# The first mixer's projections and attention waves in another order

## The chip, the cores and the metric

The program runs on one core of a Trainium2 chip. The metric is the device time of one execution in microseconds (us); the time before is the median of three runs. The engines are named PE (TensorE), ACT (ScalarE), DVE (VectorE), POOL (GpSimd) and SP (SyncE, which issues most of the DMAs). "Granted clock" is the share of full speed at which TensorE was allowed to run in a stretch: 1.00 is the upper of its two levels, 2.4 GHz, and a mean below it means that part of the stretch ran at the lower, 1.2 GHz.

## The reference, cut to what matters

Two layers, each a mixer and a feed-forward part, over 512 tokens of width 1024. The change touches the mixer of the first layer: one input projection gives the gate and the input of a recurrent unit, queries, six key and value tensors, and gates; attention sums three branches.

```python
h = modulate(x, norm_mix, sh_m, sc_m)
(a_gate, a_x, q, kc, vc, ks, vs, kw, vw, gts) = _split(h @ w_in, IN0_SIZES)
y_a = rg_lru(causal_conv(a_x, conv_w, conv_b), wa, ba, wx, bx, lam) * jax.nn.gelu(a_gate)
...
        o = gc[..., 0:1] * o_cmp + gc[..., 1:2] * o_slc + gc[..., 2:3] * o_win
...
x = x + g_m[:, None, :] * (jnp.concatenate([y_a, y_b], axis=-1) @ w_out)
```

`o_cmp` attends to 31 compressed blocks, `o_slc` to selected blocks, `o_win` to a window. With 512 tokens the selection and the window take every earlier token, so the kernel computes branches 1 and 2 as plain causal attention. The modulation values (`sh_m`, `sc_m`, `g_m` and so on) are six products of one vector with a 1024x1024 matrix.

## The kernel before

All matrix products are float32 in three passes (`passes`, L382 to L390): high part by high part (L387), low by high (L388), high by low (L389). A weight block of 1024x256 comes by one DMA of 1 MB (`load_next`, L163) into one of four buffers `raw`, is split into `whi` (ACT, L173) and `wlo` (DVE or POOL, L174), and gives two output tiles of 128x512, with 24 matmuls of 128x512 for each.

The order of the weights is the list `entries`, filled at L679: `win` (keys and values of branch 2, called the third branch in the change's name, since the compressed one is branch 0), `gts` (gates), `q0`, `q1`, `ax0`, `ax1` (recurrent input), `ag0`, `ag1` (recurrent gate), then four blocks of the output projection. `MIX_MODS` (L38) says how many blocks of the modulation matrices are loaded behind each of them; each such block costs TensorE 16 small matmuls (L256), ACT a copy `mrow` (L259) and TensorE the sum L267.

What runs when is decided by `Weaver` (L40), a co-operative scheduler: generators hand it pieces of work with estimated lengths and waits, and it writes them out by priority; a pass that follows then fixes the order on every engine. `backbone` (L1167) is the generator of the projections. It first ends the four tiles of the first two key/value blocks (banks `b_mm`, `b_mm`, `b_sc`, `b_sc`), then takes the `win` block on two banks `b_o`, then the gates (`gts_unit`, L1056), the two query blocks and the recurrent unit. Each of those tiles is emptied by ACT and DVE: `cmp_evac` (L932: `kc2`, ACT L939 and DVE L940, then `kb` on POOL, L947), `dup_k` (L1017: `khi` on ACT, `klo` on DVE) and `v_rows` (L1031: `vf` on ACT, four transposes L1040 on TensorE, the copy `vt1` or `vt2` on DVE, L1042). `compress` (L953) makes the compressed keys from `kb`.

Attention is another generator, `att_run` (L560). It works through units of one query block of 128 queries, one branch and some heads: scores into one of two banks `b_sc` (L499, L500, mask L510), maximum `negm` (DVE L515), exponential `pr` (ACT L518), normalisation (DVE L523 to L527), transposes (L534) and products with the values (L555). The list `waves` sets the order of the units: for each query block first branch 1, then branch 2. The recurrent unit is `lru1` (a convolution `xc`: ACT L865, three DVE passes L867), `lru_gates` (matmuls L875 and L877, ACT L880 and L881) and `lru2`.

Of the kernel before, what the change touches and what calls it, by code (L numbers as in the profile page):

```python
# [34 lines left out]
FFN_MODS = (((0, 1, "wu"), (0, 2, "wg"), (0, 2, "wu"), (0, 3, "wg"), (0, 0), (0, 1), (0, 2), (0, 3), (1, 0, "wg"), (1, 0, "wu"), (1, 1, "wg"), (1, 1, "wu"), (1, 2, "wg"), (1, 2, "wu"), (1, 3, "wg"), (1, 3, "wu"),   # L35
             (1, 0), (1, 1), (1, 2), (1, 3), (2, 0, "wg"), (2, 0, "wu"), (2, 1, "wg"), (2, 1, "wu"), (2, 2, "wg"), (2, 2, "wu"),  (2, 0), (2, 1)),
            ())
MIX_MODS = {'win': 0, 'gts': 0, 'q0': 2, 'q1': 1, 'ax0': 1, 'ax1': 2, 'ag0': 3, 'ag1': 2, 0: 1, 1: 0, 2: 0, 3: 0}  # L38
NPT0, OSB, NPR = 3, 2, 4
PIECES = ((4, 4, 3), (4, 4, 3))  # L40

# [56 lines left out]
def trunk(ctx, tc, I, out):  # L98
# [461 lines left out]
    def att_run(A, pre):  # L560

        flat, act, dve = [], 0.0, 0.0
        per = {0: 4, 1: 2, 2: 1, 3: 1}
        brs, ng = A["brs"], A["ng"]
        tail = brs[-1]
        waves = [(qb, w) for qb in range(NB) for w in range(0, ng, 4 if qb < 2 else 2)]
        if ng > 4:
            waves = [(qb, w) for w in (0, 4) for qb in (0, 1)] + [v for v in waves if v[0] > 1]
        for qb, w in waves:
            n, nh = per[qb], (4 if qb < 2 else 2)  # L570
            for br in brs:
                for z in range(2):
                    for h in range(w, w + nh, n):
                        hs = [z * ng + h + j for j in range(n)]
                        ev = (br, w, nh) if z == 1 and h + n == w + nh else None
                        flat.append((qb, br, z, w, h - w, nh, hs, ev))
        live, obank, pvq = {}, {}, []
        n_u = len(flat)
        for i in range(n_u + 3):
            todo, pvq = pvq, []  # L580
            if 0 <= i - 2 < n_u:
                qb, br, z, w, j0, nh, hs, ev = flat[i - 2]
                pt, W, n, ready = live.pop(i - 2)
                if ready > wv.now:
                    yield ("wait", ready - wv.now)
                pick = A["late"] is None and dve <= act
                if j0 == 0:
                    A["PT"][qb, br, w, z] = A["pool"].tile([P, 1024], F32, name="pT", tag="pT", bufs=A["npT"])[:, :nh * W]
                pe = att_T(pt, A["PT"][qb, br, w, z][:, j0 * W:(j0 + n) * W], W, n, pick)
                t0 = wv.now + pe + 100.0  # L590
                if pick:
                    dve = done = max(dve, t0) + 130.0 + n * W * 1.04
                else:
                    act = done = max(act, t0) + 220.0 + n * W * 0.83
                if ev is not None:
                    pvq = [(qb, ev, done + 100.0)]
                yield pe
            if i < n_u:
                qb, br, _, _, _, _, hs, _ = flat[i]
                for f in pre(qb, hs):  # L600
                    yield ("until", f)
                if (qb, br) in A["hooks"]:
                    wv.spawn(A["hooks"].pop((qb, br))(), -3)
                pt, pe, W, n = att_unit(A, qb, br, hs, i % 2)
                late = A["late"] is not None
                dve = max(dve, wv.now + pe + 100.0) + 130.0 + n * W * 1.04
                act = max(act, dve + 100.0) + n * (230.0 + W * 0.83)
                if i % 2 and not late:
                    dve = max(dve, act) + 400.0 + 2 * n * (100.0 + W * 0.52)
                    live[i - 1] = live[i - 1][:3] + (dve + 100.0,)  # L610
                live[i] = (pt, W, n, (act if late else dve) + 100.0)
                yield pe
            for qb, (br, w, nh), ready in todo:
                if ready > wv.now:
                    yield ("wait", ready - wv.now)
                hb = (qb, w // 4)
                if hb not in obank:
                    obank[hb] = bank("o")
                first = br == brs[0]
                if first and A["cmp"] is not None:  # L620
                    yield ("until", ("cmpo", qb))
                    yield att_PV(A, qb, 0, w, nh, obank[hb], True, False)
                    first = False
                yield att_PV(A, qb, br, w, nh, obank[hb], first, br == tail)
                if br == tail and (w + nh) % 4 == 0:
                    A["done"](qb, w // 4, obank.pop(hb))
# [48 lines left out]
    add_mod(0, 0, 2, None)  # L675
    add_mod(0, 1, 3, None)
    add_mod(0, 0, 3, None)
    for nm, c0 in (("win", 2048), ("gts", 2304), ("q0", 1024), ("q1", 1280), ("ax0", 512), ("ax1", 768), ("ag0", 0),
                   ("ag1", 256)):  # L679
        if nm == "gts":  # L680
            entries.append(("h", ("in0", nm), W0, 0, KT, c0, 24, None))
        else:
            add_w(("in0", nm), W0, 0, KT, c0, 256, (P, P))
        emit_mods(dve_mods, MIX_MODS[nm])
# [162 lines left out]
    def layer0():  # L847
# [201 lines left out]
        def kv_evac(br):  # L1049
            def f(n, o, t0, t1):  # L1050
                if n == 0:
                    dup_k(Ks, br, o, mp, "kk", 2)
                else:
                    v_rows(Vs, br, o, mp, "xc", 2)
            return f
# [76 lines left out]
        def done(qb, half, o):  # L1132
# [6 lines left out]
                 cmp=lambda qb, i: (CK["v"][:, i % 2].rearrange("p z d -> p (z d)"),  # L1139
                                    PCT[qb][:, (i // 2) * P:(i // 2 + 1) * P]),  # L1140
                 late=None, hooks={(qb, 1): (lambda qb=qb: cmp_block(qb)) for qb in range(NB)})
        wv.spawn(att_run(A, lambda qb, hs: [("q", 7), "gts", "cmp"]), -1)

        def ag_evac(ft, o):
            ag = mp.tile([P, S], F32, name="ag", tag="xc", bufs=2)
# [19 lines left out]
        sq_ = stack_q(Qs, mp, "qs", 8, 0.125, lambda h: h // 4)  # L1165

        def backbone():  # L1167
            need(("in0", "win"))
            for n, ev in enumerate((cmp_evac, kv_evac(1))):
                for z in range(2):  # L1170
                    for k in kv_g[2 * n + z]:
                        yield 3 * MM
                    ev(z, kv_o[2 * n + z], 0, S)
            for y in pair(("in0", "win"), KT, 2, rh, rl, ("o", "o"), kv_evac(2)):
                yield y
            wv.set("kv2", CMP_WAIT)
            for y in gts_unit(("in0", "gts")):
                yield y
            for j in range(2):
                def qe(n, o, t0, t1, j=j):  # L1180
                    sq_(4 * j + 2 * n, o)
                    wv.set(("q", 4 * j + 2 * n), 2000.0)
                    wv.set(("q", 4 * j + 2 * n + 1), 2500.0)
                for y in pair(("in0", "q%d" % j), KT, 2, rh, rl, T2, qe):
                    yield y
            for j in range(2):
                for y in pair(("in0", "ax%d" % j), KT, 2, rh, rl, T2, lambda n, o, t0, t1, j=j: lru1(2 * j + n, o)):
                    yield y
                if j:
                    yield ("until", ("lru", 0))  # L1190
                for ft in (2 * j, 2 * j + 1):
                    yield ("until", ("xc", ft))
                    for y in lru_gates(ft):
                        yield y
                wv.spawn(lru2(j), -4)
# [243 lines left out]
    def layer1():  # L1439
# [88 lines left out]
        def done(qb, half, o):  # L1528
# [5 lines left out]
            for p in range(4):  # L1534
                for z in range(2):
# [8 lines left out]
        A = dict(pool=mp, npr=3, bias=BIAS, K=Ks, Q=Qs, V=Vs, PT={}, npT=3, ng=8, grp=lambda h: h // 8, done=done, brs=(3,),  # L1544
                 gate=None, cmp=None, hooks={},
                 late=[mp.tile([P, 16], F32, name="rr%d" % qb) for qb in range(NB)])
        wv.spawn(att_run(A, lambda qb, hs: [("q", hs[-1], 1), "kv"] + ([("bias", qb)] if qb else [])), -1)
        wv.spawn(idx_scores(), -2)
        sqi = stack_q(Qi, mp, "lq", 16, 1.0, lambda h: 0)
        sq_ = stack_q(Qs, mp, "lq", 16, 0.125, lambda h: h // 8)  # L1550
# [68 lines left out]
```

## Time and profile before

| what | before |
|---|---|
| median of three runs | 1300.6 us (1300.31 to 1300.71) |
| the profiled execution, its own time | 1300.9 us |
| its span in the trace | 1299.1 us |
| mean granted clock | 0.993 |
| busy: PE, DVE, ACT, POOL | 1256.4, 769.3, 506.0, 267.4 us |
| chain that ended last | PE 81%, DVE 11%, ACT 4% |

Read it from the top: TensorE is busy for 97% of the span, and four fifths of the chain that ended last is its work. The other engines are busy for 59% or less of the span, but not evenly. The first mixer lies at about 50 to 280 us. In the rows of the timeline a bracket gives the idle time of the engine ahead of an instruction and what ended it.

### The profile page before, as it was taken

The page shows a single profiled execution, that of the slowest core. Times are in us where ns is not written, and L with a number is a line of the kernel's source. Part 1 is how long each engine was busy: PE and PEld are TensorE (multiplying, and loading weights), DVE is VectorE, ACT ScalarE, POOL GpSimd, SP SyncE. Part 2 cuts the span into 40 slices and gives each one's busy share as a digit, 9 for nine tenths or more (in the row PEclk, how much of TensorE's full clock was granted, in tenths as well). Part 3 has the DMA queues.
Part 4 walks back from the last instruction along what each step waited for, and adds up shares of the span by engine and source line. Part 5 has one row for each costly group of instructions (what it writes and reads, how often), then busy time and mean ns, then how long its engine had stood idle before and what let it go on. Part 6 is the DMA issues. An engine that isn't in the chain of part 4 may idle for free.

```text
span 1299.1 us, 17835 instructions
## 1 busy us (share of the span) xinstructions
PE 1256.4 (97%) x7024; PEld 1042.5 (80%) x7024; DVE 769.3 (59%) x1482; ACT 506.0 (39%) x935; POOL 267.4 (21%) x213
## 2 busy tenths in 40 slices
PE   6999999999999999999999998999999999999997
PEld 4777676789888888888898777778988888888886
DVE  6455877758655567656657699954833333333434
ACT  3444765534322222212234546773432222222323
POOL 2310142011225335344323522003000000000003
PEclk9999999999999999999998999999999999999999
DMA  9854123423535555555542523002232333233201
GB/s 325 258 166 146 60 69 98 135 93 98 163 130 162 173 175 172 194 194 193 172 131 65 130 43 78 11 2 66 66 98 98 97 98 97 97 97 97 99 15 65
DMA packets 151651, 153.52 MB, mean 118 GB/s; under 512 B 6632, under 2 KB 149136, under 8 KB 151568
## 3 DMA queue, kind: packets, MB, share of 16 engines
q1 hardware_dynamic: 150560, 151.24, 37.3%
q8 instruction: 55, 0.90, 0.3%
q10 hardware_dynamic: 656, 1.08, 0.2%
q14 instruction: 28, 0.23, 0.1%
q0 software_dynamic: 352, 0.07, 0.0%
HBM read 150.28 MB, written 2.10 MB: 117 GB/s over the span
## 4 chain that ended last, share of the span: by engine, by line
PE 81%; DVE 11%; ACT 4%; SPq 2%; DMA 2%; issue 1%; POOLq 0%; POOL 0%; ACTq 0%; DVEq 0%
PE b_mm L387 12%; PE b_mm L388 12%; PE b_mm L389 12%; PE b_sc L387 10%; PE b_sc L388 9%; PE b_sc L389 9%; PE b_o L555 2%; PE b_tp L534 2%; DVE isc L1504 2%; SPq L163 1%; DVE m L1503 1%; PE b_sc L499 1%; DMA raw<-in_l_mod_w 1%; PE b_tp L256 1%; ACT pr L518 1%
## 5 line engine op out<-in xcount | busy, mean ns | idle before, releaser
L173 ACT ACTIVATE whi<-raw 128x1024 fp32r<-128x1024 f32 (+1 forms) x175 | 182.4, 1047 | 497.6 <-PE b_mm L388 193.2
L174 DVE TENSOR_TENSOR wlo<-raw,whi 128x1024 fp32r<-128x1024 f32 (+1 forms) x148 | 197.0, 1334 | 136.7 <-ACT whi L173 134.7
L387 PE MATMUL b_mm<-fh,whi 128*128 128x512 f32 x320 | 126.4, 395 | 0.0
L387 PE MATMUL b_sc<-fh,whi 128*128 128x512 f32 x320 | 124.8, 390 | 0.0
L388 PE MATMUL b_mm<-fl,whi 128*128 128x512 f32 x320 | 124.6, 389 | 0.0
L389 PE MATMUL b_sc<-fh,wlo 128*128 128x512 f32 x320 | 124.6, 389 | 0.0
L388 PE MATMUL b_sc<-fl,whi 128*128 128x512 f32 x320 | 124.5, 389 | 0.0
L389 PE MATMUL b_mm<-fh,wlo 128*128 128x512 f32 x320 | 124.5, 390 | 0.0
L285 POOL TENSOR_TENSOR raw<-raw,silu_c 128x1024 f32<-128x1024 f32 x28 | 60.2, 2171 | 230.5 <-DMA raw<-in_l_mod_w 146.5
L174 POOL TENSOR_TENSOR wlo<-raw,whi 128x1024 fp32r<-128x1024 f32 (+1 forms) x27 | 65.0, 2419 | 148.9 <-ACT whi L173 146.7
L1279 DVE TENSOR_TENSOR sg<-sg,b_sc 128x512 f32<-128x512 f32 (+1 forms) x48 | 30.6, 642 | 99.9 <-PE b_sc L389 99.9
L1406 POOL TENSOR_TENSOR xall<-xall,raw 128x512 f32<-128x512 f32 (+1 forms) x9 | 10.5, 1166 | 379.8 <-ACT ftmp L1405 379.8
L387 PE MATMUL b_mm<-hhi,whi 128*128 128x512 f32 x208 | 82.5, 401 | 1.7 <-DVE qs L1012 1.0
L389 PE MATMUL b_mm<-hhi,wlo 128*128 128x512 f32 x208 | 82.3, 395 | 0.0
L388 PE MATMUL b_mm<-hlo,whi 128*128 128x512 f32 x208 | 82.1, 395 | 0.0
L288 POOL TENSOR_TENSOR raw<-raw 128x1024 f32<-128x1024 f32 (+2 forms) x42 | 76.4, 1820 | 3.3
L389 PEld LDWEIGHTS b_mm<-fh,wlo 128*128 128x128 f32 x320 | 60.1, 188 | 13.0
L389 PEld LDWEIGHTS b_sc<-fh,wlo 128*128 128x128 f32 x320 | 60.1, 188 | 12.6
L387 PEld LDWEIGHTS b_sc<-fh,whi 128*128 128x128 f32 x320 | 60.1, 188 | 12.4
L388 PEld LDWEIGHTS b_sc<-fl,whi 128*128 128x128 f32 x320 | 60.1, 188 | 12.3
L388 PEld LDWEIGHTS b_mm<-fl,whi 128*128 128x128 f32 x320 | 60.2, 188 | 12.0
L387 PEld LDWEIGHTS b_mm<-fh,whi 128*128 128x128 f32 x320 | 60.1, 188 | 12.0
(380 smaller groups left out, 2971.5 us busy)
## 6 DMA issues: line engine op xcount, KB each, us to landing
raw<-in_l_mod_w SPq DMA_DIRECT2D x42, 1024.0 KB, 5.3
raw<-in_l_ffn_wg SPq DMA_DIRECT2D x22, 1024.0 KB, 5.4
raw<-in_l_ffn_wu SPq DMA_DIRECT2D x22, 1024.0 KB, 7.6
raw<-in_l_ffn_wd SPq DMA_DIRECT2D x19, 1024.0 KB, 5.0
raw<-in_l_w_in SPq DMA_DIRECT2D x16, 1024.0 KB, 5.3
rawm<-in_l_mod_w SPq DMA_DIRECT2D x6, 1024.0 KB, 11.2
raw<-in_l_w_out SPq DMA_DIRECT2D x12, 512.0 KB, 5.1
raw<-in_l_ffn_wd SPq DMA_DIRECT2D x4, 768.0 KB, 6.7
```

The lines of the kernel that those rows point to most:

```text
L163: nc.sync.dma_start(v[:, :k0], I[name][r0:r0 + k0 * P, cs].rearrange("(k p) n -> p k n", p=P))
L173: nc.scalar.activation(hi, raw, AF.Copy)
L174: (eng or nc.vector).tensor_tensor(lo, raw, hi.bitcast(F32), op=OP.subtract)
L285: nc.gpsimd.tensor_tensor(raw[:, k:k + 4], raw[:, k:k + 4], sc_c[:, k:k + 4][:, :, None].to_broadcast([P, 4, 256]), op=OP.mult)
L288: nc.gpsimd.tensor_tensor(raw[:, 0:n], raw[:, 0:n], raw[:, n:2 * n], op=OP.add)
L387: mm(o, hi[:, k], rhi(k), start=(start and k == 0), stop=False)
L388: mm(o, hi[:, k], rlo(k), start=False, stop=False)
L389: mm(o, lo[:, k], rhi(k), start=False, stop=(stop and k == nk - 1))
L534: nc.tensor.transpose(b[:, j * P:(j + 1) * P], pt[:, j * P:(j + 1) * P], ident)
L555: mm(o[64 * z:64 * z + 64, cs].rearrange("p (h q) -> p h q", h=nh), v[:, kb, z * 64:(z + 1) * 64], pT[z][:, :, kb * P:(kb + 1) * P], start ...
L1279: nc.vector.tensor_tensor(t, t, o, op=OP.mult)
L1504: nc.vector.match_replace(sc_, m8, sc_, SENT)
```

## The change

The weight list now runs `gts`, `q0`, `q1`, `win`, `ax0`, and so on; `backbone` takes the `win` pair after both query blocks, on the banks `b_mm`, and sets a flag `kvw` behind it. The modulation blocks (12, as before) are loaded behind `ax0` (2), `ax1` (3), `ag0` (3), `ag1` (3) and the first output block (1), where they were behind `q0`, `q1` and so on. The attention of query blocks 0 and 1 goes branch 1 of both first, then branch 2 of both (which waits for `kvw`); query blocks 2 and 3 stay as they were. No computation is added or left out; the second layer's line only gets the new argument.

```diff
-MIX_MODS = {'win': 0, 'gts': 0, 'q0': 2, 'q1': 1, 'ax0': 1, 'ax1': 2, 'ag0': 3, 'ag1': 2, 0: 1, 1: 0, 2: 0, 3: 0}
+MIX_MODS = {'win': 0, 'gts': 0, 'q0': 0, 'q1': 0, 'ax0': 2, 'ax1': 3, 'ag0': 3, 'ag1': 3, 0: 1, 1: 0, 2: 0, 3: 0}
...
-        waves = [(qb, w) for qb in range(NB) for w in range(0, ng, 4 if qb < 2 else 2)]
         if ng > 4:
-            waves = [(qb, w) for w in (0, 4) for qb in (0, 1)] + [v for v in waves if v[0] > 1]
-        for qb, w in waves:
+            waves = [(qb, w, brs) for w in (0, 4) for qb in (0, 1)]
+        else:
+            waves = [(qb, 0, (br,)) for br in brs for qb in (0, 1)]
+        for qb, w, bs in waves + [(qb, w, brs) for qb in (2, 3) for w in range(0, ng, 2)]:
             n, nh = per[qb], (4 if qb < 2 else 2)
-            for br in brs:
+            for br in bs:
...
-                for f in pre(qb, hs):
+                for f in pre(qb, br, hs):
...
-    for nm, c0 in (("win", 2048), ("gts", 2304), ("q0", 1024), ("q1", 1280), ("ax0", 512), ("ax1", 768), ("ag0", 0),
+    for nm, c0 in (("gts", 2304), ("q0", 1024), ("q1", 1280), ("win", 2048), ("ax0", 512), ("ax1", 768), ("ag0", 0),
                    ("ag1", 256)):
...
-        wv.spawn(att_run(A, lambda qb, hs: [("q", 7), "gts", "cmp"]), -1)
+        wv.spawn(att_run(A, lambda qb, br, hs: [("q", 7), "gts", "cmp"] + (["kvw"] if br == 2 else [])), -1)
...
-            need(("in0", "win"))
+            need(("in0", "gts"))
...
-            for y in pair(("in0", "win"), KT, 2, rh, rl, ("o", "o"), kv_evac(2)):
-                yield y
             wv.set("kv2", CMP_WAIT)
...
+            for y in pair(("in0", "win"), KT, 2, rh, rl, T2, kv_evac(2)):
+                yield y
+            wv.set("kvw", 3500.0)
```

What this does to the order of instructions is shown at three places. The first is TensorE where the first two key/value blocks end (`b_sc` from `kvw`, the split weights of the second block). Before, the last of them and what follows; 28 matmuls into `b_o` (the `win` block) stand ahead of the transposes L1040, and 20 more stand earlier:

```order
L388 MATMUL b_sc<-hlo,kvw 128x512
L389 MATMUL b_sc<-hhi,kvw 128x512
L387 MATMUL b_o<-hhi,whi 128x512
L388 MATMUL b_o<-hlo,whi 128x512
L389 MATMUL b_o<-hhi,wlo 128x512
L387 MATMUL b_o<-hhi,whi 128x512
```

Now:

```order
L388 MATMUL b_sc<-hlo,kvw 128x512
L389 MATMUL b_sc<-hhi,kvw 128x512
L1041 MATMUL b_tp<-ident,vf 128x128 x4
L1063 MATMUL b_mm<-hhi,whl 48x512
L1064 MATMUL b_mm<-hlo,whl 48x512
```

All 48 matmuls of the `win` block have gone from there; the transposes and the gates' matmuls follow the key/value tiles at once.

The second is DVE at the same place (buffer numbers tell `kc2_621` and `kc2_622`, the two copies of the first bank, apart). Before, from the two small memsets on:

```order
L966 MEMSET hid0_775 128x64
L966 MEMSET hid1_802 128x256
L940 COPY kc2_621<-b_mm_456 64x511
L1028 TENSOR_TENSOR klo_658<-b_sc_458,khi_657 64x512
L855 CAST cmask_574<-cm_575 128x128
L174 TENSOR_TENSOR wlo_749<-raw_324,whi_748 128x1024
L1028 TENSOR_TENSOR klo_708<-b_o_675,khi_707 64x512
L940 COPY kc2_622<-b_mm_456 64x511
```

Now:

```order
L967 MEMSET hid0_696 128x64
L967 MEMSET hid1_723 128x256
L174 TENSOR_TENSOR wlo_780<-raw_324,whi_779 128x1024
L941 COPY kc2_621<-b_mm_456 64x511
L1029 TENSOR_TENSOR klo_658<-b_sc_458,khi_657 64x512
L856 CAST cmask_574<-cm_575 128x128
L1043 COPY vt1_741<-b_tp_736 128x512
L941 COPY kc2_622<-b_mm_456 64x511
```

`kc2_622`, which frees the first bank for the gates' matmuls, has five instructions ahead of it since the memsets in both, now with `vt1` among them.

The third place is between the recurrent blocks `ax0` and `ax1`. On DVE before, where the values of branch 2 (`vt2`) are copied, in the middle of `compress`:

```order
L968 COPY hx_801<-b_o_784 128x62
L969 TENSOR_TENSOR hx_801<-hx_801 128x62
L1042 COPY vt2_820<-b_tp_815 128x512
L970 TENSOR_SCALAR hx_801<-hx_801 128x62
L984 TENSOR_TENSOR ck_828<-b_o_826,ck_828 128x2x32
```

DVE now; `psum_1254`, `pr_1252` and `pr_1276` belong to branch 2 of query block 0:

```order
L523 RECIPROCAL psum_1254<-psum_1254 128x8
L524 SCALAR_TENSOR_TENSOR psum_1254<-psum_1254,gates_581 128x8
L527 TENSOR_SCALAR pr_1252<-pr_1252,psum_1254 128x128 x4
L527 TENSOR_SCALAR pr_1276<-pr_1276,psum_1254 128x128 x4
L515 TENSOR_REDUCE negm_1336<-b_sc_1331 128x2
L868 SCALAR_TENSOR_TENSOR xc_1452<-b_mm_1381,V2_91,xc_1452 128x511
L1043 COPY vt2_1229<-b_tp_1224 128x512
L515 TENSOR_REDUCE negm_1364<-b_sc_1359 128x2
```

The copy of `vt2` has moved from the compression into the attention, behind ten instructions on probabilities, a maximum and a convolution pass.

TensorE around that copy, now (there is no such place before):

```order
L1041 MATMUL b_tp_1224<-ident_73,vf_1189 128x128 x4
L499 MATMUL b_sc_1359<-khi_1028,qs_845 128x256
L500 MATMUL b_sc_1359<-klo_1029,qs_845 128x256
L499 MATMUL b_sc_1359<-khi_1028,qs_848 128x256
L500 MATMUL b_sc_1359<-klo_1029,qs_848 128x256
L510 MATMUL b_sc_1359<-cmask_574,identr_78 128x2x128
L267 MATMUL b_tp_1211<-quarter_82,mrow_1220 128x1 x2
L534 MATMUL b_tp_1232<-ident_73,pr_1150 128x128 x4
L534 MATMUL b_tp_1260<-ident_73,pr_1175 128x128 x4
```

`b_tp` has two banks that take turns, so `b_tp_1232` uses the bank of `b_tp_1224` again, and stands right behind one unit of scores and one small sum. TensorE at the end of the mixer (`b_o` is the last query block's output; `b_mm_2751` and the like are the output projection) had this before:

```order
L555 MATMUL b_o_2362<-pT_2701,vt2_820 64x256
L555 MATMUL b_o_2362<-pT_2617,vt2_820 64x256
L387 MATMUL b_mm_2751<-yhi_2473,whi_2179 128x256
L387 MATMUL b_sc_2752<-yhi_2473,whi_2183 128x256
L387 MATMUL b_mm_2817<-yhi_2473,whi_2507 128x256
L387 MATMUL b_sc_2818<-yhi_2473,whi_2511 128x256
```

Now (`b_mm_2751` follows twelve of these rows later):

```order
L555 MATMUL b_o_2238<-pT_2569,vt2_1229 64x256
L555 MATMUL b_o_2238<-pT_2507,vt2_1229 64x256
L267 MATMUL b_tp_2637<-quarter_82,mrow_2646 128x1 x2
L387 MATMUL b_sc_2818<-yhi_2590,whi_2614 128x256
L388 MATMUL b_sc_2818<-ylo_2591,whi_2614 128x256
L389 MATMUL b_sc_2818<-yhi_2590,wlo_2615 128x256
L387 MATMUL b_sc_2818<-yhi_2590,whi_2614 128x256
L388 MATMUL b_sc_2818<-ylo_2591,whi_2614 128x256
```

Twelve matmuls of the output projection that need only the recurrent half (`b_sc_2818`) have moved behind the last attention product.

## Rows read from the trace of the kernel before

**Rows 1.** The page: busy time of the engines, the chain, DMA issues (KB, us to landing)

```profile
PE 1256.4 (97%) x7024; PEld 1042.5 (80%) x7024; DVE 769.3 (59%) x1482; ACT 506.0 (39%) x935; POOL 267.4 (21%) x213
...
PE 81%; DVE 11%; ACT 4%; SPq 2%; DMA 2%; issue 1%; POOLq 0%; POOL 0%; ACTq 0%; DVEq 0%
...
raw<-in_l_mod_w SPq DMA_DIRECT2D x42, 1024.0 KB, 5.3
```

**Rows 2.** Timeline, TensorE, 51 to 69 us: start, length, engine, line, operation, shapes, idle before

```profile
51.17 0.39 PE L387 MATMUL b_o<-hhi,whi 128*128 128x512 f32 x1
...
61.15 0.39 PE L387 MATMUL b_o<-hhi,whi 128*128 128x512 f32 x1
...
67.50 0.60 PE L1040 MATMUL b_tp<-ident,vf 128*128 128x128 f32 x4
68.35 0.44 PE L1062 MATMUL b_mm<-hhi,whl 128*48 128x512 f32 x1 [0.25 <-DVE kc L940]
```

**Rows 3.** Timeline, DVE, the same stretch

```profile
61.40 0.39 DVE L966 MEMSET hid<- 128x64 f32 x2 [0.45 <-PE b_sc L389]
62.02 0.68 DVE L940 COPY kc<-b_mm 64x511 f32<-64x511 f32 x1 [0.24 <-ACT kc L939]
63.11 0.68 DVE L1028 TENSOR_TENSOR klo<-b_sc,khi 64x512 fp32r<-64x512 f32 x1 [0.40 <-ACT khi L1027]
64.14 1.70 DVE L855 CAST cmask<-cm 128x128 fp32r<-128x128 f32 x1 [0.35 <-POOL cm L737]
65.76 1.21 DVE L174 TENSOR_TENSOR wlo<-raw,whi 128x1024 fp32r<-128x1024 f32 x1
...
69.77 0.69 DVE L1042 COPY vt<-b_tp 128x512 f32<-128x512 f32 x1
```

**Rows 4.** Timeline, ACT and POOL, the same stretch

```profile
63.10 0.60 ACT L1034 ACTIVATE vf<-b_sc 128x512 f32<-128x512 f32 x1
...
64.33 1.42 POOL L947 TENSOR_TENSOR kb<-kc,V 128x248 f32<-128x248 f32 x2
```

**Rows 5.** Timeline, TensorE, three places where its clock fell soon after

```profile
688.67 0.86 PE L337 MATMUL b_tp<-ident,nr 128*128 128x128 f32 x4 [1.61 <-DVE nr L331]
...
811.49 0.33 PE L499 MATMUL b_sc<-khi,qs 128*128 128x128 f32 x1 [2.28 <-DVE qs L1012]
...
890.38 0.39 PE L387 MATMUL b_mm<-yhi,whi 128*128 128x256 f32 x1 [1.53 <-ACT yhi L1523]
```

**Rows 6.** Stretches of 20 us: busy time of each engine, PEclk, DMA share, GB/s

```profile
680.00:700.00 20.00, 17.71 (x120) 17.19 (x119) 17.46 (x55) 8.04 (x16) 8.58 (x4) 0.83 0.34 106
800.00:820.00 20.00, 15.96 (x102) 13.02 (x101) 19.52 (x64) 14.83 (x42) 4.77 (x2) 0.91 0.17 53
880.00:900.00 20.00, 18.47 (x148) 16.79 (x145) 6.49 (x12) 8.72 (x16) 6.08 (x5) 0.91 0.00 1
```

**Rows 7.** Timeline, ACT: first and last of one unit's four exponentials

```profile
123.03 0.37 ACT L518 ACTIVATE pr<-b_sc,negm 128x128 f32<-128x128 f32 x1 [1.94 <-DVE negm L515]
...
124.32 0.21 ACT L518 ACTIVATION_READ_ACCUMULATOR pr<-b_sc,negm 128x1 f32 x1
```

**Rows 8.** Timeline, DVE: a convolution pass, a maximum, a pair's eight scalings

```profile
131.16 0.74 DVE L867 SCALAR_TENSOR_TENSOR xc<-b_mm,V,xc 128x509 f32<-128x509 f32 x1
...
132.70 0.69 DVE L515 TENSOR_REDUCE negm<-b_sc 128x2 f32<-128x512 f32 x1
...
133.96 1.66 DVE L527 TENSOR_SCALAR pr<-pr,psum 128x128 f32<-128x128 f32 x8
```

**Rows 9.** Timeline, TensorE: its larger waits in the first mixer

```profile
130.00 1.13 PE L877 MATMUL b_mm<-xc,bd_wx 128*128 128x512 f32 x2 [0.84 <-ACT lr L880]
...
208.63 0.44 PE L499 MATMUL b_sc<-khi,qs 128*128 128x384 f32 x1 [0.88 <-ACT pr L518]
...
222.59 0.39 PE L387 MATMUL b_mm<-yhi,whi 128*128 128x256 f32 x1 [1.38 <-ACT whi L173]
...
276.00 0.39 PE L387 MATMUL b_mm<-yhi,whi 128*128 128x256 f32 x1 [1.36 <-ACT yhi L1128]
```

More of the change, by code (lines that the diff above doesn't have):

```diff
@@ L1546, in layer1 @@
                  late=[mp.tile([P, 16], F32, name="rr%d" % qb) for qb in range(NB)])
-        wv.spawn(att_run(A, lambda qb, hs: [("q", hs[-1], 1), "kv"] + ([("bias", qb)] if qb else [])), -1)
+        wv.spawn(att_run(A, lambda qb, br, hs: [("q", hs[-1], 1), "kv"] + ([("bias", qb)] if qb else [])), -1)
         wv.spawn(idx_scores(), -2)
```

## The prediction

> **What bounds the kernel now.** I read the page's busy times first: TensorE works for 1256.4 us of a span of 1299.1, and 81% of the chain that ended last is its own work; no other engine passes 59% [rows 1]. The change adds and removes no matmul, so a busy time cannot move the end; only TensorE's idle time and its clock can. The timeline of TensorE comes next. In the first mixer the larger waits are 0.84, 0.88, 1.38 and 1.36 us [rows 9]; these make 4.5, and with the smaller ones, below 0.75 each, I add up some 6.3 us of idle time between 110 and 280 us. That is the most that a better order there can give back, half a per cent. Before 110 us there is nearly none: the `win` block's matmuls run without a gap up to the transposes at 67.50, and the gates' matmuls start at 68.35 after a wait of 0.25 [rows 2]. So I ask two things: what fills TensorE where `win` leaves, and what fills it where attention now comes.
>
> **Step 1, the gap that `win` leaves: +4.8 us.** The key/value tiles end at 61.15 [rows 2]; call this K. In before TensorE then has 28 matmuls of `win` at 0.227 us, 6.35 us of work (61.15 to 67.50), while ACT and DVE empty the four banks. Now only the transposes (0.60) and the gates' matmuls are left, and these need the bank that `kc2_622` frees. DVE's order gives the chain ahead of it: the memsets wait for the last key/value matmul and start at K+0.25 (61.40), then come memsets 0.39, `wlo` 1.21, `kc2_621` 0.68, `klo` 0.68, the cast of the mask 1.70, `vt1` 0.69 and `kc2_622` 0.68 [rows 3]: K+6.3. ACT is not later: `vf` is ready at 63.70, K+2.55 [rows 4], and the transposes 0.6 after it. TensorE works for 0.60 of those 6.3, so it idles 5.7, against 0.25: +5.4. The cast is the open term. Its 1.70 us lie beside the POOL instruction `kb`, 64.33 to 65.75, and it ends just after that [rows 3, 4]; `klo` has four times its columns and took 0.68. Without that company I put it at 0.4 (estimate, between nothing and the 0.68 of `klo`), and the term is +4.1. Which of the two starts first is a matter of a tenth of a microsecond here (`klo` ends at K+3.2, where POOL also comes free), so I take the middle, +4.8.
>
> The Trainium skill ("SBUF — State Buffer", section "Who interferes with whom") says that DVE and GpSimd share one pair of ports under an exclusive lock, and that whichever instruction comes first keeps the other waiting for its whole length. In the trace here the cast started at 64.14, ahead of `kb` at 64.33, and yet it was the long one, so the order of recorded starts does not bear out who should wait. By that rule a cast that truly comes first would be short, and this term alone would be +4.1 and the whole sum 0.7 lower.
>
> The 20 `win` matmuls that stood at 51.17 [rows 2] leave no large hole: the key/value matmuls behind them move up. The gates' matmuls and `compress` keep their order behind; one modulation block of 1 MB now stands between the compression's weights on SP's queue, where such a block takes 5.3 us to land [rows 1]. The weights are used some 9 us after the key/value tiles end, so I cost it at nothing; without that cover it is up to 1.
>
> **Step 2, the clock: +1.7 us.** The gap of step 1 comes in two parts, about 2.5 us for `vf` and 3 for the bank, less than a microsecond apart. In before TensorE's clock fell soon after waits of 1.61, 2.28 and 1.53 us [rows 5], while behind the 1.36 at 276.00 [rows 9] it held. The stretches with the three falls show a mean granted clock of 0.83, 0.91 and 0.91 [rows 6]: of 20 us, 6.8, 3.6 and 3.6 ran at the lower level of 1.2 GHz. Where TensorE has dense work, half of that is lost, 3.4 or 1.8. Behind our gap stand the gates and `compress`, dense: I take one short fall, +1.7, with 0 and 3.4 as ends.
>
> **Step 3, branch 2 inside the attention: +3.7 us.** Branch 2's keys and values were ready before attention began; now they are made in it. The price is read at `vt2`. TensorE's transposes `b_tp_1232` need the bank that the copy `vt2` empties. That copy stands on DVE behind the normalisation of the unit whose exponential `pr_1276` is the last to come. From the end of that exponential DVE needs the two small instructions (0.4 together, estimate from their neighbours of 0.2 or less), eight scalings 1.66, `negm` 0.69, one pass of `xc` 0.74 [rows 8] and the copy 0.69 [rows 3]: 4.2 us. The same exponential frees a bank for the scores that TensorE has ahead of `b_tp_1232`: five matmuls of 256 columns, half of the 0.227 of 512 columns each, and two tiny ones, about 0.9 us. So TensorE waits about 3 us there. Further, a unit's four exponentials take 123.03 to 124.53, 1.5 us [rows 7], and with two banks for scores TensorE has only 0.6 to 1.1 us of scores per unit between them; before, backbone matmuls lay between, now `ax1` stands behind the whole group. I count three waits of half a microsecond, 1.5. Less the 0.84 that this place costs in before [rows 9]: +3.7. The ends are 0 (DVE and ACT arrive early, or the copy finds other work of TensorE's beside it) and +6 (each unit's exponentials in full).
>
> **Step 4, the end of the mixer: -1.4 us.** At 276.00 TensorE waits 1.36 for the last attention output [rows 9]. Now twelve output-projection matmuls of 256 columns (0.114 each, by half of 0.227) that don't need it stand there, 1.4 us of work: the wait is covered. The other late waits, 0.88 and 1.38 [rows 9], have the same kind of work around them as before; I leave them. Against this, the second output block's weights are now loaded behind a modulation block: 5.3 us to land [rows 1] less the first block's 24 matmuls (2.7) could stall it for up to 2.6. Ends: -4.9 (all late waits gone) and +1.2.
>
> The moved modulation blocks are 12 before and after; their matmuls stay beside the backbone, at the same price. The modulation value for the mixer's output is needed only when the output projection ends, with all its blocks ahead.
>
> **The sum.** 4.8 + 1.7 + 3.7 - 1.4 = +8.8 on the profiled execution's 1300.9, so 1309.7; the median lies 0.3 below that execution, so I say 1309.4.
>
> **The rivals.** *Faster.* Attention starts over 10 us earlier (48 `win` matmuls of 0.227 and the modulation blocks no longer stand ahead of the queries), so its chains of exponentials spread over more backbone work and every wait of the mixer disappears: 1300.6 - 6.3 + 4.1 = 1298.4, with a short cast and no fall of the clock. It decides once steps 1 and 3 together cost less than the waits that vanish. For it speaks that the late waits are all on ACT or DVE; against it, that steps 1 and 3 follow from the order itself. 0.05. *Within noise.* Step 1 at its lower end, clock held, step 3 at zero and half of the late waits gone: 1300.6 + 4.1 - 3 = 1301.7. 0.12. *Only the start counts.* ACT and DVE keep up in the attention, step 3 at zero: 1300.6 + 4.8 + 1.7 - 1.4 = 1305.7. For it speaks that DVE is busy for 59% of the span only [rows 1], against it the ten DVE instructions ahead of `vt2`. 0.25. *The clock falls twice*, behind `vt2` also (its 3 us are longer than any of the three waits that did it), and the output weights come late: 1309.4 + 1.7 + 2.6 = 1313.7. 0.20. *The change doesn't do what it says*: the order of instructions shows that it does; no chance.
>
> **How the numbers follow.** My forecast has 0.38. A run of this kernel can be told from no change beyond about 0.2%, 2.6 us. Faster 0.05, the same 0.12, slower 0.83. The range leaves out the faster case and about half of the case within noise below, and above only a clock fall at its long price on top of the fourth rival: 1302 to 1316.
>
> **What would show it.** Step 1: TensorE idle for about 5 us in two waits just ahead of the gates' matmuls, on ACT `vf` and DVE `kc`, near 57 to 63 us. Step 2: a granted clock below 1 in the 20 us behind. Step 3: a wait of 2 to 3.5 us on DVE `vt` at the transposes between `ax0` and `ax1`, and no such wait if DVE arrives early. Step 4: no wait ahead of the output projection's last part. It would be wrong if the first gap were filled by matmuls that the order puts later, or if the late waits vanished one and all.

## The result and the profile after

| what | before | after |
|---|---|---|
| median | 1300.59 us | 1310.85 us (1309.31 to 1312.79, 4 runs) |
| ratio to before, 95% interval | | 1.008 (1.0068 to 1.0092) |
| span of the profiled execution | 1299.1 us | 1308.7 us |
| mean granted clock | 0.993 | 0.984 |

The change makes the kernel 10.3 us slower, well outside what a measurement of this kernel can confuse with no change. The prediction was 1309.4 us. The busy times say little, as they did before [rows 1]; the first row is that of the busy times, the second the chain that ended last:

```profile
PE 1259.7 (96%) x7024; PEld 1045.6 (80%) x7024; DVE 763.6 (58%) x1482; ACT 504.1 (39%) x933; POOL 263.4 (20%) x213
...
PE 82%; DVE 10%; ACT 3%; DMA 3%; issue 1%; SPq 0%; POOLq 0%; POOL 0%; DVEq 0%; ACTq 0%
```

TensorE does the same 7024 instructions and is 3.3 us busier for them, at a lower mean clock (0.984 against 0.993); the other 6 us are idle time. The place where it happens can be read by comparing the same point of the two programs. The first matmul of the first feed-forward part that waits for `sg` stands, in the timeline of TensorE before and after, at:

```profile
322.33 0.39 PE L439 MATMUL b_mm<-fh,whi 128*128 128x256 f32 x1 [1.34 <-ACT sg L1273]
```

```profile
333.76 0.39 PE L439 MATMUL b_mm<-fh,whi 128*128 128x256 f32 x1 [1.34 <-ACT sg L1275]
```

It is 11.4 us later. All of the loss is made by then; the rest of the program gives 1.8 us back (9.6 in the span). From this row on TensorE has the same 4982 instructions in all twelve kernels that were traced for this document, and they take between 972.3 and 977.2 us; the 976.8 of before and the 974.9 of after lie inside that. Where the clock falls there differs from trace to trace (below).

**Ahead of the gates.** TensorE after, from the last key/value matmul to the compression; these rows answer to [rows 2]:

```profile
57.64 0.39 PE L389 MATMUL b_sc<-hhi,kvw 128*128 128x512 f32 x1
60.76 0.63 PE L1041 MATMUL b_tp<-ident,vf 128*128 128x128 f32 x4 [2.74 <-ACT vf L1035]
63.25 0.66 PE L1063 MATMUL b_mm<-hhi,whl 128*48 128x512 f32 x1 [1.86 <-DVE kc L941]
63.71 0.63 PE L1064 MATMUL b_mm<-hlo,whl 128*48 128x512 f32 x1
...
66.60 0.39 PE L1063 MATMUL b_mm<-hhi,whl 128*48 128x512 f32 x1
```

Two waits, 2.74 for `vf` and 1.86 for `kc`, where there was 0.25. Behind them the matmuls start 0.43 us apart and take 0.63; from 66.60 on they take the 0.39 of before. The compression, which follows the gates, starts at 72.10 before and at 68.45 after:

```profile
72.10 7.25 PE L961 MATMUL b_o<-kb,w1t 128*128 128x62 f32 x64
```

```profile
68.45 7.25 PE L962 MATMUL b_o<-kb,w1t 128*128 128x62 f32 x64
```

DVE and POOL in that stretch answer to [rows 3, 4]; the first two `kb`, which a wider window of the timeline merges into one row, are shown one by one:

```profile
57.57 1.23 DVE L174 TENSOR_TENSOR wlo<-raw,whi 128x1024 fp32r<-128x1024 f32 x1 [3.89 <-ACT whi L173]
58.76 0.39 DVE L967 MEMSET hid<- 128x64 f32 x2
59.06 1.16 DVE L174 TENSOR_TENSOR wlo<-raw,whi 128x1024 fp32r<-128x1024 f32 x1
60.25 0.68 DVE L941 COPY kc<-b_mm 64x511 f32<-64x511 f32 x1
60.96 0.68 DVE L1029 TENSOR_TENSOR klo<-b_sc,khi 64x512 fp32r<-64x512 f32 x1
61.57 0.30 DVE L856 CAST cmask<-cm 128x128 fp32r<-128x128 f32 x1
61.80 0.67 DVE L1043 COPY vt<-b_tp 128x512 f32<-128x512 f32 x1
62.50 1.41 DVE L941 COPY kc<-b_mm 64x511 f32<-64x511 f32 x2
```

```profile
61.07 0.72 POOL L948 TENSOR_TENSOR kb<-kc,V 128x248 f32<-128x248 f32 x1
61.76 0.71 POOL L948 TENSOR_TENSOR kb<-kc,V 128x248 f32<-128x248 f32 x1
```

DVE works through the chain without a pause from 57.57, and TensorE waits for the second `kc`. The cast took 0.30 us this time: it started within POOL's first `kb` and ended at 61.87, 0.08 us behind that `kb`'s end at 61.79.

**Between `ax0` and `ax1`.** TensorE and DVE around the copy of `vt2`:

```profile
139.19 0.50 PE L267 MATMUL b_tp<-quarter,mrow 128*128 128x1 f32 x4
141.57 1.97 PE L534 MATMUL b_tp<-ident,pr 128*128 128x128 f32 x8 [1.87 <-DVE vt L1043]
```

```profile
138.00 1.66 DVE L527 TENSOR_SCALAR pr<-pr,psum 128x128 f32<-128x128 f32 x8
139.58 0.68 DVE L515 TENSOR_REDUCE negm<-b_sc 128x2 f32<-128x512 f32 x1
140.18 0.74 DVE L868 SCALAR_TENSOR_TENSOR xc<-b_mm,V,xc 128x511 f32<-128x511 f32 x1
140.83 0.68 DVE L1043 COPY vt<-b_tp 128x512 f32<-128x512 f32 x1
```

**In the attention of the last two query blocks.** TensorE's larger waits there; they answer to the rows from 208 us on in [rows 9]. Below them ACT and DVE at the second and the third:

```profile
201.06 0.50 PE L387 MATMUL b_mm<-hhi,whi 128*128 128x512 f32 x1 [1.31 <-ACT whi L173]
...
231.29 0.80 PE L499 MATMUL b_sc<-khi,qs 128*128 128x512 f32 x1 [1.93 <-ACT pr L518]
...
234.70 0.69 PE L1114 MATMUL b_tp<-ident,cpc 128*128 128x128 f32 x2 [2.08 <-DVE cpc L1110]
...
261.82 0.38 PE L387 MATMUL b_mm<-yhi,whi 128*128 128x256 f32 x1 [1.69 <-ACT whi L173]
```

```profile
222.95 1.70 ACT L1162 ACTIVATE yhi<-lr 128x512 fp32r<-128x512 f32 x3
224.51 1.17 ACT L1129 ACTIVATE yhi<-os 128x512 fp32r<-128x512 f32 x2
...
228.91 0.63 ACT L1129 ACTIVATE yhi<-os 128x512 fp32r<-128x512 f32 x1
229.79 0.63 ACT L1162 ACTIVATE yhi<-lr 128x512 fp32r<-128x512 f32 x1 [0.25 <-DVE lr L1154]
230.46 0.69 ACT L518 ACTIVATE pr<-b_sc,negm 128x512 f32<-128x512 f32 x1
```

```profile
225.80 1.76 DVE L1163 SCALAR_TENSOR_TENSOR ylo<-lr,yhi 128x512 fp32r<-128x512 f32 x2
227.49 1.28 DVE L1130 TENSOR_TENSOR ylo<-os,yhi 128x512 fp32r<-128x512 f32 x2
...
234.24 0.41 DVE L1110 TENSOR_TENSOR cpc<-cpc,crr 128x256 f32<-128x256 f32 x1
```

The exponential that frees a bank for TensorE at 231 stands behind seven splits of the mixer's output into high and low parts (`yhi`), and the product `cpc` for which TensorE waits at 234.70 comes on DVE behind as many `ylo`. In the kernel before, the first of these splits ran 20 us earlier:

```profile
202.81 1.67 ACT L1161 ACTIVATE yhi<-lr 128x512 fp32r<-128x512 f32 x3
```

Stretches of 20 us of the changed kernel show what the clock did (PE, PEld, DVE, ACT, POOL busy, then the mean granted clock, DMA share, GB/s):

```profile
60.00:80.00 20.00, 17.38 (x107) 13.85 (x108) 8.66 (x21) 6.44 (x14) 6.59 (x11) 0.91 0.71 208
...
140.00:160.00 20.00, 18.43 (x98) 13.06 (x99) 13.88 (x30) 15.03 (x32) 3.17 (x4) 0.91 0.41 131
...
220.00:240.00 20.00, 15.54 (x115) 10.63 (x114) 16.12 (x42) 12.29 (x30) 3.65 (x3) 0.76 0.33 107
...
900.00:920.00 20.00, 18.47 (x153) 17.75 (x150) 11.61 (x15) 7.37 (x12) 10.21 (x6) 1.00 0.32 100
```

In the first mixer, where the clock held throughout before, it falls three times: at the waits ahead of the gates, at the one for `vt2`, and at those of 231 to 235 us.

### The profile page after: what moved, and what is told of

Same layout as the page of the kernel before. It is cut to its first block, busy times and chain, and to the rows that moved or that the text cites. A ratio compares the mean times of both kernels' runs of the same rounds, so it can differ in the third digit from the quotient of the medians.

```text
span 1308.7 us, 17831 instructions
## 1 busy us (share of the span) xinstructions
PE 1259.7 (96%) x7024; PEld 1045.6 (80%) x7024; DVE 763.6 (58%) x1482; ACT 504.1 (39%) x933; POOL 263.4 (20%) x213
## 4 chain that ended last, share of the span: by engine, by line
PE 82%; DVE 10%; ACT 3%; DMA 3%; issue 1%; SPq 0%; POOLq 0%; POOL 0%; DVEq 0%; ACTq 0%
PE b_mm L387 12%; PE b_mm L388 12%; PE b_mm L389 12%; PE b_sc L387 10%; PE b_sc L389 9%; PE b_sc L388 9%; DMA raw<-in_l_w_in 2%; PE b_o L555 2%; PE b_tp L534 2%; DVE isc L1506 1%; DVE m L1505 1%; PE b_tp L256 1%; PE b_sc L499 1%; DMA raw<-in_l_w_out 1%; PE b_sc L500 1%; DVE isc L1490 1%
## 5 line engine op out<-in xcount | busy, mean ns | idle before, releaser
L387 PE MATMUL b_mm<-hhi,whi 128*128 128x512 f32 x224 | 89.2, 403 | 2.7 <-ACT whi L173 1.3
L388 PE MATMUL b_mm<-hlo,whi 128*128 128x512 f32 x224 | 88.6, 396 | 0.0
L389 PE MATMUL b_mm<-hhi,wlo 128*128 128x512 f32 x224 | 88.0, 394 | 0.0
```

The source lines that it names most:

```text
L387: mm(o, hi[:, k], rhi(k), start=(start and k == 0), stop=False)
L388: mm(o, hi[:, k], rlo(k), start=False, stop=False)
L389: mm(o, lo[:, k], rhi(k), start=False, stop=(stop and k == nk - 1))
```

## The experiments

Each kernel was timed beside the kernel before on its own chip, so the ratios are compared, not the times. "Idle late" is the sum of TensorE's idle time from 190 to 300 us, added up from its timeline: 5.3 us before, 7.9 after.

**Is it the empty place ahead of the gates? (e4)** The first query block is put where the `win` block was, on `b_o`. The diff is against the changed kernel.

```diff
-    for nm, c0 in (("gts", 2304), ("q0", 1024), ("q1", 1280), ("win", 2048), ("ax0", 512), ...
+    for nm, c0 in (("q0", 1024), ("gts", 2304), ("q1", 1280), ("win", 2048), ("ax0", 512), ...
...
+            for y in qpair(0, ("o", "o")):
+                yield y
             wv.set("kv2", CMP_WAIT)
```

> The changed kernel with one difference: the first query block takes the place that the win block had in the kernel before (two b_o banks, ahead of the gates), so that TensorE has 48 matmuls that need no bank of the key/value tiles. Theory: the 4.6 us of idle time ahead of the gates and the fall of the clock behind it (1.6 to 1.7 us) come from the empty place alone; both go, and the time is 1310.9 - 4.6 - 1.7 = 1304.6, 1303 to 1306. Rival: the banks are emptied no sooner whatever stands there, the wait only moves to the gates: 1309 to 1311.

Measured: ratio 1.0016 (1.0005 to 1.0026), median 1302.34. TensorE at the gates:

```profile
68.02 0.43 PE L1063 MATMUL b_mm<-hhi,whl 128*48 128x512 f32 x1 [0.25 <-DVE kc L941]
```

The wait is 0.25, as before, and the clock in 60 to 80 us is 1.00. From 1.008 to 1.0016 is 0.64% or 8.3 us, a little more than the 6.3 expected; the intervals allow 5.5 to 11. So most of the loss is the place that nothing filled, and the rival falls: the banks are emptied at the same pace, and other work hides it.

**The new order of the weights alone (e11).** Waves and modulation blocks as before; again against the changed kernel.

```diff
-            waves = [(qb, 0, (br,)) for br in brs for qb in (0, 1)]
+            waves = [(qb, 0, brs) for qb in (0, 1)]
...
-MIX_MODS = {'win': 0, 'gts': 0, 'q0': 0, 'q1': 0, 'ax0': 2, 'ax1': 3, 'ag0': 3, 'ag1': 3, 0: 1, 1: 0, 2: 0, 3: 0}
+MIX_MODS = {'win': 0, 'gts': 0, 'q0': 2, 'q1': 1, 'ax0': 1, 'ax1': 2, 'ag0': 3, 'ag1': 2, 0: 1, 1: 0, 2: 0, 3: 0}
```

> The kernel before with only the new place of the win block (entries, backbone, the flag); waves and modulation blocks as before. Theory: the idle time of 4.6 us ahead of the gates and the fall of the clock behind it (1.7) are the cost of the new place wherever the rest stands, and the rest of the mixer changes by no more than 2 us either way: ratio 1.0033 to 1.0065, some 6.3 us. Rival: a good part of that is given back later in the mixer, because ACT and DVE are ahead: ratio at most 1.002.

Measured: 1.0062 (1.005 to 1.0075), 1308.70. The time is in the theory's range: the new order alone makes most of the loss, 0.62 of 0.80%. TensorE ahead of the gates, and the stretch around it:

```profile
60.81 1.09 PE L1041 MATMUL b_tp<-ident,vf 128*128 128x128 f32 x4 [2.75 <-ACT vf L1035]
63.41 0.66 PE L1063 MATMUL b_mm<-hhi,whl 128*48 128x512 f32 x1 [1.51 <-DVE kc L941]
```

```profile
60.00:80.00 20.00, 17.68 (x115) 13.20 (x115) 8.79 (x21) 6.50 (x14) 6.62 (x11) 0.83 0.74 211
```

The waits are those of the changed kernel within 0.4 us, but the transposes are slow already (1.09 against 0.63) and the clock's mean is 0.83: it fell earlier here, and stayed down for 6.8 us in place of 3.4. But the start is not all of it. TensorE also has two late waits, for splits of the mixer's output, and idle late is 7.8:

```profile
230.25 0.38 PE L387 MATMUL b_mm<-yhi,whi 128*128 128x256 f32 x1 [3.27 <-ACT yhi L1162]
...
233.26 0.58 PE L388 MATMUL b_mm<-ylo,whi 128*128 128x256 f32 x1 [2.63 <-DVE ylo L1163]
```

This trace reaches the feed-forward part at 332.61, 10.3 us later than the kernel before, and 7.85 of that is there when the compression starts. So the mixer behind the start changes by 2.4 us, a little more than the theory's 2, and the total fits because the rest of the program is 3 us shorter in this trace (973.8 against 976.8).

**The `win` block back, the rest of the change kept (e1).** Entries and pair as before; waves and modulation blocks of the change.

```diff
+            for y in pair(("in0", "win"), KT, 2, rh, rl, ("o", "o"), kv_evac(2)):
+                yield y
+            wv.set("kvw")
             wv.set("kv2", CMP_WAIT)
...
```

> The changed kernel with the win block back where it was (first, on b_o banks); the waves by branch and the later modulation blocks stay. Theory: the gap ahead of the gates, the wait for vt2 and the clock falls behind both go; what is left is the late part of the mixer, which is 2.9 us more idle time and a fall of the clock there: 1300.6 + 2.9 + up to 3 = 1303.5 to 1306.5. Rival: the late part is also a consequence of the win block's place, all of the loss goes: 1300 to 1301.5.

Measured: 0.9996 (0.9984 to 1.0007), 1300.09. The rival is right: with the `win` block back nothing of the loss is left. Idle late is 6.2, and the splits start at 203.56, as in the kernel before.

**The modulation blocks alone (e2).** One line of the change, `MIX_MODS`, in the kernel before.

> The kernel before with only the new places of the modulation blocks. Theory: the late waits of the changed kernel (1.9 and 2.1 us near 231 to 235, 1.7 at 262) come from the modulation blocks that now fall into the attention of the last two query blocks and ahead of the second output block: 1303 to 1306 here. Rival: they come from the attention's order, and the modulation blocks can stand anywhere: 1300 to 1301.5.

Measured: 0.9988 (0.9977 to 0.9998), 1298.38. The time lies under both ranges, nearer to the rival's, and the trace speaks for a part of the theory. TensorE's largest wait there:

```profile
235.92 0.58 PE L387 MATMUL b_mm<-yhi,whi 128*128 128x256 f32 x1 [3.43 <-ACT whi L173]
```

It waits 3.43 us for the second output block's weights, and yet the kernel is not slower. Smaller waits went (idle from 100 to 190 us is 0.6 in place of 1.5), but not all of it is made up in the mixer: this trace reaches the feed-forward part at 323.23, 0.9 us later than before, and the rest of the program is 2.0 us shorter in it.

**The waves alone (e3).** The list `waves` of the change in the kernel before.

> The kernel before with only the new waves (branch 1 of query blocks 0 and 1, then branch 2 of both). Theory: the order of the units by itself costs nothing, since the win block is ready before attention starts: 1299.5 to 1301.5. Rival: the waves by branch make the late waits, 1303 or more.

Measured: 1.0026 (1.0013 to 1.004), 1304.44. The theory that the order of the units is free falls. One wait that it makes lies between the recurrent blocks, and two are late, as the rival has it:

```profile
132.76 0.39 PE L499 MATMUL b_sc<-khi,qs 128*128 128x256 f32 x1 [1.83 <-ACT pr L518]
...
209.67 0.55 PE L534 MATMUL b_tp<-ident,pr 128*128 128x128 f32 x3 [1.87 <-DVE pT L536]
...
227.64 0.39 PE L387 MATMUL b_mm<-yhi,whi 128*128 128x256 f32 x1 [2.28 <-ACT whi L173]
```

In the kernel before, these three places waited 0.27, 0.70 and 1.38; idle late is 7.2. Together with the modulation blocks of the change (e1) the same waves cost nothing, so the two parts are not a sum.

**The change with the old modulation blocks (e6).** `MIX_MODS` of before in the changed kernel.

> The changed kernel with the old places of the modulation blocks (behind the same names). Theory: in the changed kernel the later modulation blocks are a help, as e1 against e3 shows (1300.1 to 1304.4, both with the new waves): 1310.9 + 4 = 1315, 1312.5 to 1317. Rival: they are a cost or nothing here, since the late waits stand beside them: 1306 to 1311.

Measured: 1.0067 (1.0045 to 1.0089), 1309.38. The theory falls: 1315 is far off, and the places of the modulation blocks make no difference that shows here. In its trace the wait at `vt2` is gone (the recurrent gates' matmuls L876 and L878 stand ahead of those transposes), and instead TensorE waits 3.01 us at 234.87 for an output block's `whi`.

**Branch 2 ready before attention (e9).** The kernel of e4 with `win` ahead of the second query block; the diff is against e4.

```diff
-    for nm, c0 in (("q0", 1024), ("gts", 2304), ("q1", 1280), ("win", 2048), ("ax0", 512), ...
+    for nm, c0 in (("q0", 1024), ("gts", 2304), ("win", 2048), ("q1", 1280), ("ax0", 512), ...
```

> The kernel of e4_query_filler with the win block one place earlier, ahead of the second query block, so that branch 2 has its keys and values before attention starts. Theory: the wait of the transposes for vt2 (1.88 us at 133.8 in e4) and the 1.24 us at 143.8 go: 1302.3 - 3.1 = 1299.2, 1298 to 1301. Rival: the group of units between the recurrent blocks waits for exponentials anyway, and the wait moves to another row: 1302 or more.

Measured: 1.0022 (1.0013 to 1.0032), 1303.33. The wait at `vt2` went, as expected, and the time did not: 60 us later there are two new ones.

```profile
201.46 0.45 PE L499 MATMUL b_sc<-khi,qs 128*128 128x384 f32 x1 [1.34 <-ACT pr L518]
205.24 0.69 PE L499 MATMUL b_sc<-khi,qs 128*128 128x384 f32 x1 [2.54 <-ACT pr L518]
```

The rival is right that the wait moves, though it moved much further than it said.

**Modulation blocks away from the output blocks (e7, e10, e12).** Three kernels. In the kernel before, the block behind the first output block goes behind `q1`, the rest as in the change (e7); the same places in the kernel of e9 (e10); and all blocks ahead of `ag1` (e12, the last line):

```diff
-MIX_MODS = {'win': 0, 'gts': 0, 'q0': 2, 'q1': 1, 'ax0': 1, 'ax1': 2, 'ag0': 3, 'ag1': 2, 0: 1, 1: 0, 2: 0, 3: 0}
+MIX_MODS = {'win': 0, 'gts': 0, 'q0': 0, 'q1': 1, 'ax0': 2, 'ax1': 3, 'ag0': 3, 'ag1': 3, 0: 0, 1: 0, 2: 0, 3: 0}
...
+MIX_MODS = {'win': 0, 'gts': 0, 'q0': 2, 'q1': 2, 'ax0': 2, 'ax1': 3, 'ag0': 3, 'ag1': 0, 0: 0, 1: 0, 2: 0, 3: 0}
```

> The kernel of e2_mods_only with the one modulation block that was loaded behind the first output block put behind the second query block. Theory: the wait of 3.43 us at 235.9 in e2 is for the second output block's weights, which stand behind that modulation block on SP's queue; it goes, and the fall of the clock behind it (3.4 us at the lower level, 1.7): 1298.4 - 3.4 - 1.7 = 1293.3, 1292 to 1296. Rival: the buffer for these weights comes free too late in any case: 1298 or more.

> The kernel of e9_win_second with the modulation blocks placed as in e7_mods_no_out. Theory: the stall of the second output block's weights is the same in this order, so it gains 1 to 4 us over e9: 1296 to 1299. Rival: the weights are not late with this order of the attention, same as e9 within 1 us.

> The kernel before with all modulation blocks loaded ahead of the recurrent gate's second block (2 behind q0, 2 q1, 2 ax0, 3 ax1, 3 ag0, none behind ag1 and the output blocks). Theory: the waits for the output projection's weights (3.43 us in e2, 2.02 in e7, both on ACT whi from the DMA) come from modulation blocks that hold the four load buffers just before them; with none there they go: 1297.9 - 2.0 - 1.7 for the clock = 1294, ratio 0.994 to 0.9965. Rival: the buffers come free by the attention's pace and the wait stays: same as e7, 0.9975 to 0.999.

Measured: e7 0.9978 (0.9968 to 0.9987), 1297.89; e10 1.005 (1.0035 to 1.0065), 1307.12; e12 1.0041 (1.0027 to 1.0054), 1306.00. The first is between theory and rival: the wait for the weights is 2.02 us in place of 3.43, and this is the fastest kernel here. Its trace shows no gain in the mixer, though: it reaches the feed-forward part at 322.65, 0.3 us later than the kernel before, so what makes it faster stays open. e10 is slower than e9 and fits neither. In e12 no matmul waits for `whi` in the mixer any more, as its theory says, and the kernel is slower all the same, since TensorE now waits more among the matmuls of the attention:

```profile
197.94 0.55 PE L534 MATMUL b_tp<-ident,pr 128*128 128x128 f32 x3 [1.20 <-ACT pT L538]
...
224.92 0.55 PE L534 MATMUL b_tp<-ident,pr 128*128 128x128 f32 x3 [1.34 <-DVE mod L244]
```

The trace also has a wait of 2.95 us at 248.15 for `cpc`. Idle late is 10.0 against 5.3. So the late modulation blocks look to be both a nuisance, for the load buffers, and work that TensorE can do while it waits for exponentials.

## Why the prediction held, point by point

**Step 1, the gap (+4.8): right, 4.7, by two misses that cancel.** The waits are 2.74 + 1.86 + 0.31 (for `hhi`, before the last group of key/value matmuls; the prediction left it out) less 0.25. The chain on DVE was named rightly, but it starts 0.6 us later, because another `wlo` (57.57) stood ahead of the memsets, and the cast took 0.30, not the half-way value of about 1. The condition that the prediction gave for the cast was wrong: it ran beside a `kb` here too, and was short, since it came late in the first of the two. e4, where other work stands in that place, and e11, where nothing else was changed, show that the empty place is the cause.

**Step 2, the clock (+1.7): right.** From 63.25 to 66.60 TensorE started eight matmuls in 3.35 us, which take 1.85 at the 0.231 of the rows behind: 1.5 lost. In the sum of both steps: the gates begin at 63.25 with 48 matmuls of `win` (10.9 us) still to do, which is 5.8 later than at 68.35 with them done, and the compression 7.25 later (68.45 against 72.10 in the timeline). Of that, 0.65 was there at 51 us already, before the order differs (in this execution the mean clock from 20 to 40 us is 0.83, in the kernel before 1.00), and 6.6 is the two steps, against 6.5.

**Step 3, branch 2 (+3.7): the mechanism right, the size too large.** The wait at `vt2` is there, on the copy that was named and behind the same instructions, but it is 1.87, not 3. DVE needed nearly the 4.2 us that were worked out: 4.0, from the end of the last exponential and its sum at 137.53 to the end of the copy at 141.51. The term that was mis-sized is TensorE's own work in that time. The prediction gave it 0.9 us; it had the previous unit's scores and four transposes still to do, and was busy until 139.69, for 2.2. The three further waits of half a microsecond did not come; the only other one up to 190 us is 0.41, for `pT`, at 170.73. Between 100 and 190 us the idle time grew from 1.5 to 2.3, by 0.8. The clock fell there too, as the fourth rival said: the eight transposes took 1.97 us, where the same number at 154.57 took 1.04.

**Step 4, the end of the mixer (-1.4): wrong.** The wait of 1.36 ahead of the output projection's last part is gone, as predicted. But idle late rose from 5.3 to 7.9 us, where the prediction left "the other late waits" as they were, and the clock fell there for 10 us. The step that failed is that sentence. The waits of 1.31 and 1.69 are for weights behind modulation blocks: the prediction saw the second as an end of the range, and in its fourth rival, and did not take it. Those of 1.93 and 2.08 come where the splits of the mixer's output crowd ACT and DVE; in the kernel before, these started at 202.81 and here at 222.95. The traces say with what part of the change this comes: the splits start at 202 to 205 us in e1, e2, e3 and e7, which have the `win` block first and the new waves, the new places of the modulation blocks or both, and at 218 to 230 in e6 and e11, with `win` behind both query blocks. So in the changed kernel it is the place of `win` again, as e1 has it (with all modulation blocks early, in e12, they start at 215.5 too). By what path it delays the splits is not shown; the trace of the changed kernel shows that the recurrent gate's last weights came late (201.06), and the split overwrites the buffers that these matmuls read.

**The sum.** By the feed-forward part 11.4 us were lost: 7.25 by the compression (forecast 6.5) and 4.2 behind it (forecast 2.3: 3.7 - 1.4). The total came within 1.5 us because the rest of the program gave 1.8 back. That was not forecast, and it is luck and no effect of the change: the same instructions and waits stand there, and they take 972.3 to 977.2 us over the twelve traces. Steps 3 and 4 missed in opposite directions besides: between 100 and 190 us the idle time grew by 0.8 where 3.7 was forecast, and late it grew by 2.6 where 1.4 was to go.

**The rivals.** "Only the start counts" is the larger part and not the whole: the start made 7.25 of the 11.4 us, and in e11 7.85 of 10.3. "The clock falls twice" had both of its events right, the fall at `vt2` and the late output weights (1.69, not 2.6); its sum was too high, since it stood on the too large step 3. "Faster" needed the late waits to vanish; they grew. Where waits go when one is removed was the weak side of the prediction and of the experiments: e7, e9 and e12 each removed or shortened the wait that they named, and the time missed the theory's range in all three; e3, e6 and e10 missed it as well.

## What to carry to other kernels

Before a block of work is moved, ask what it covers where it stands: 48 matmuls that needed none of the banks being emptied were worth 6.6 us there, and another block of that kind in the place, the first query block, brought most of the loss back. Where a co-operative scheduler interleaves several generators, the cost of a hole at the start can be read from the order and the durations; the waits that appear later can't be added up part by part, and a small change of the order should be timed, not reasoned. A wait of 2 us on a busy TensorE costs more than its length when the clock falls behind it, as at `vt2`. And two programs are best compared at the first common instruction behind the changed part: what followed here varied by 5 us with the same instructions.

## What the runs showed of the hardware

The clock does not answer to the same wait in the same way. In the kernel before it fell soon after the wait of 1.53 us for `yhi` [rows 5, 6]; in the changed kernel, after the same wait, it held, and the stretch from 900 to 920 us shows 1.00:

```profile
902.30 0.39 PE L387 MATMUL b_mm<-yhi,whi 128*128 128x256 f32 x1 [1.53 <-ACT yhi L1525]
```

At the gap ahead of the gates it fell for 3.4 us in the changed kernel and for 6.8 in e11. Among 54 runs of the kernel before that stood beside the experiments, the eleven with a mean granted clock of 0.989 took 1302.2 us on average and the eighteen with 0.992 took 1299.9. The scatter of the changed kernel's four runs is not explained by that mean: 0.984 goes with 1309.31 and with 1312.79.

The cast of a 128x128 mask on DVE took 1.70 us in the kernel before, where it started at 64.14, just ahead of POOL's two `kb` [rows 3, 4], and ended at 65.84, 0.09 behind the end of the second, whose row is:

```profile
65.02 0.73 POOL L947 TENSOR_TENSOR kb<-kc,V 128x248 f32<-128x248 f32 x1
```

In the changed kernel it took 0.30: it started half a microsecond into the first `kb` and ended 0.08 behind that one's end. In the other ten traces, too, it ends some 0.08 us behind the end of one of the two. The Trainium skill ("SBUF — State Buffer", section "Who interferes with whom") says that whichever of the two issues first gets the ports that they share for its whole length, and that the other waits, where the DVE instruction is in one of its 2-port modes. The changed kernel agrees with that: the cast came second and ended when the first `kb` was over. The kernel before doesn't by its recorded starts, since there the cast came first by 0.19 us and yet was the one that lasted until both `kb` were over; no run here tells why.
